# Memory keys behind the latent heads' transposes, paired products at a stage's entry, residual sums with priority

## The chip, the cores and the metric

The kernel runs on one core of a Trainium2 chip. The metric is the device time of one execution in microseconds (us). Engines are named as in the profile: PE is the matrix engine's multiplication, PEld its weight load, DVE the vector engine, ACT the scalar engine, POOL the GpSimd engine, SP the engine whose queue issues the weight loads.

## The reference, cut to what matters

Two transformer blocks run one after the other on an input of 256 tokens by 1024 features, in fp32. In short:

```
x = x + 0.5 * swiglu(norm(x), W1)                   # stage ffn1, hidden width 2816
z = norm(x) @ w_in + b_in                           # stage mix: sliding-window attention, mLSTM
x = x + merged(attention, mlstm, gates) @ w_out
x = x + 0.5 * swiglu(norm(x), W2)                   # stage ffn2
x = norm(x)
x = x + concat(gated_linear_attention, latent_attention) @ w_out_2     # stage mix2
x = x + cross_attention(norm(x), norm(mem)) @ xa_w_o                   # part xa of mix2
x = x + (silu(conv3(norm(x) @ w_gate)) * (norm(x) @ w_up)) @ w_down    # stage ffn3
```

In mix2 the latent attention has 8 heads of 96 query and key features. The cross attention of xa has 4 heads of 128; its keys are a product of the 256 memory tokens with a 1024 by 512 matrix and do not depend on x. The norm's gain is multiplied into x before a product; the factor of the norm that differs by token is applied to the product.

## The kernel before, in words

The activations lie transposed, as eight feature tiles `x[0]` to `x[7]` of 128 features by 256 tokens. Every fp32 matrix product is made from halves: an operand is split into a high part that the fast fp32 format holds, and the remainder. `x_done(d)` (line 462) splits feature tile d with the next norm's gain: ACT writes the high part (line 480), DVE the low part (line 481). `halves` (line 346) does the same for a piece of weights: ACT writes `wh` (line 354), DVE writes `wl` (line 355); there are six buffers of each, a piece holds 1024 columns, and in mix2 and the first two products of ffn3 it is written in two instructions of 512 columns. Raw weights come by SP's queue into three buffers `wr`.

`mm3` (line 374) is one step of a product over one feature tile: two instructions, one of 512 columns and one of 256 (lines 382 and 383). `lin_t` (line 391) makes two output tiles j = 0, 1 over eight feature tiles k, 16 such steps, into one buffer of the PSUM pool `mm`, which has two. `lin_n` (line 401) makes a product with tokens as rows, by three instructions of 512 columns for each feature tile and token block (lines 387 to 389). The pool `at` has four PSUM banks; scores, transposes, small sums and the first product of a stage use it.

`lin_first` (line 418) makes the first product of a stage, whose feature tiles have only just been written: for both j the first six feature tiles, then the last two. In ffn2 and ffn3 that is the gate product `g0`, followed by `lin_t` for the up product `u0`; in mix it is `aq00`, followed by `aq01`. At the end of mix, `wo0` to `wo3` (line 914) multiply the merged heads `gs`, which are written two feature tiles at a time as the products `pm0` to `pm3` end (lines 906 to 910); `joined` (line 534) empties a product's PSUM by ACT (line 540) and DVE (line 541).

In `mix2_heads`, `turned(hp)` (line 1163) transposes the queries `q` and keys `kn` of one pair of latent heads on PE (line 1169, four transposes each) and copies them out as `qT` (DVE, line 1172) and `kT` (ACT, line 1174). `scores(qT, hp)` multiplies them (lines 1184, 1185), and `values` the rows after the softmax. The source has turned(0), scores(0), turned(1), then the products og and uv, scores(1), turned(2), the product gv, then `xa_memory` and values(0), and then `xa_keys` (line 1376): the memory keys `xk`, a `lin_n` of 48 instructions over eight feature tiles, squares (line 1386), a reciprocal root on POOL, a multiplication (line 1390). `xa_turn` transposes the result on PE (line 1399).

In `xa` (line 1407), `values(0)` (line 1468) stands right behind the memory values `xv` (line 1405). Then come turn(1) (line 1460), norm(3) (line 510), scores(3) (line 1442), and the output products xo0 and xo1, each followed by four additions to x (lines 1507 and 1513) and `x_done`.

The instructions are not issued in the order of the source. A planner simulates the program with its own times for each instruction, and gives each engine a fixed list: of what is ready in its simulation, the instruction that stands first in the source. On the chip each engine works off its list and waits on semaphores.

Of the kernel before, what the change touches and what calls it, by code (L numbers as in the profile page):

```python
# [2 lines left out]

# [1 line left out]

# [10 lines left out]
ALU = mybir.AluOpType  # L16
# [171 lines left out]
class Builder:  # L188
# [209 lines left out]
                self.mm3(ps[:, j, :], hv[j][0][:, k, :], hv[j][1][:, k, :], xs[k], k == 0, k == kt - 1)  # L398
        return ps

    def lin_n(self, key, n, xs, kt=KD, pool=None):

        ps = [(pool or self.bank)() for _ in range(TB)]
        for k, kk, runs in n_runs(n, kt):
            raw = self.wraw(f"{key}.{k}")
            for s, m in runs:
                hi, lo = self.halves(raw[:, s * n:(s + m) * n])
                for i in range(m):
                    q = k + s + i
                    for b in range(TB):  # L410
                        self.mm3n(ps[b][:, :n], xs[q][:, 0, b * P:b * P + P], xs[q][:, 1, b * P:b * P + P],
                                  hi[:, i * n:i * n + n], lo[:, i * n:i * n + n], q == 0, q == kt - 1)
        return ps

    def xtiles(self, k):
        return self.xp.tile([P, 2, T], F32R, tag=f"xs{k}", name=self.n(f"xs{k}"))

    def lin_first(self, key, xs, raw=None):


        ps = [self.pa() for _ in range(2)]
        if raw is None:
            hv = self.wcols(key, 2)
            for ks in (range(6), range(6, 8)):
                for j in range(2):
                    for k in ks:
                        self.mm3(ps[j], hv[j][0][:, k, :], hv[j][1][:, k, :], xs[k], k == 0, k == 7)
        else:
            for q in range(4):
                for d in (2 * q, 2 * q + 1):  # L430
                    self.x_done(d)
                    xs.append(self.halved[d])
                hl = [t[:, :512].rearrange("p (j k c) -> p j k c", j=2, k=2) for t in self.halves(raw[:, q * 512:q * 512 + 512])]
                for j in range(2):
                    for k in range(2):
                        self.mm3(ps[j], hl[0][:, j, k, :], hl[1][:, j, k, :], xs[2 * q + k],
                                 q + k == 0, q + k == 4)
        return ps


# [106 lines left out]
    def ffn(self, f, half, nxt=None, conv=False, last=False, first=False, mem=False):  # L547
# [3 lines left out]
        with self.phase("ffn") as fp:  # L551
            ft = lambda shape, tag, bufs=1, dt=F32: fp.tile(shape, dt, tag=tag, name=self.n(tag), bufs=bufs)
            xs = [] if first else self.split_x()
            ahl = ft([P, 2, KF, T], "ahl", dt=F32R)
            pairs = {}

            def products(pr):
                if pr == 0:
                    pg = self.lin_first(f"{f}g{pr}", xs, self.first if first else None)
                else:  # L560
                    pg = self.lin_t(f"{f}g{pr}", xs)
                if conv:
                    s = ft([P, 2, T + 2], "g", 2)
                    nc.vector.memset(s[:, :, 0:2], 0.0)
                    self.joined(pg, s[:, :, 2:])
                else:
                    s = ft([P, 2, T], "s", 2)
                    self.joined(pg, s)
                a = ft([P, 2, T], "a", 2)
                self.joined(self.lin_t(f"{f}u{pr}", xs, early=first and pr == 0), a)  # L570
                pairs[pr] = s, a

            if not first:
                acc = self.squares(self.x2)
            products(0)
            if first:
                acc = self.squares(self.x2, True)
            rN, _ = self.rinv_n(self.mean(acc, "ms"))
            products(1)
            self.fine = 1  # L580
            if first:
                self.ip = fp
                self.consts2()
                self.rope_tables()
            r = self.by_token(rN)
            rh = ft([P, T], "rh")
            nc.vector.tensor_scalar(rh, r, 0.5 if half else 1.0, None, ALU.mult)
            for pr in range(KF // 2):
                if pr > 1:
                    products(pr)  # L590
                s, a = pairs.pop(pr)
                if conv:
                    g, s = s, ft([P, 2, T], "s", 2)
                    nc.vector.tensor_tensor(g[:, :, 2:], g[:, :, 2:], self.bc2(r), ALU.mult)
                    for j in range(2):
                        w = [self.col("cw3", 22 * t + 2 * pr + j) for t in range(3)]
                        nc.scalar.activation(s[:, j, :], g[:, j, 2:], AF.Identity, scale=w[2], bias=self.col("cb3", 2 * pr + j))
                        for t in (1, 0):
                            nc.vector.scalar_tensor_tensor(s[:, j, :], g[:, j, t:T + t], w[t], s[:, j, :], ALU.mult, ALU.add)
                else:  # L600
                    nc.vector.tensor_tensor(s, s, self.bc2(r), ALU.mult)
                nc.scalar.activation(s, s, AF.Silu)
                nc.vector.tensor_tensor(a, s, a, ALU.mult)
                self.split(ahl[:, :, 2 * pr:2 * pr + 2, :], a)
            if mem:
                self.xa_norm()
            if nxt is not None:
                self.then(nxt)
            for dp in range(KD // 2):
                short = dp == KD // 2 - 1  # L610
                ps = self.pm()[:, :, :T if short else 2 * T]
                for k0, kt in balanced(KF, 8):
                    hv = self.wcols(f"{f}d{dp}.{k0}", 2, kt)
                    for j in range(2):
                        for k in range(kt):
                            q = k0 + k
                            self.mm3(ps[:, j, :], hv[j][0][:, k, :], hv[j][1][:, k, :], ahl[:, :, q, :],
                                     q == 0, q == KF - 1)
                y = ft([P, 2, T], "dy", 2)
                if not short:  # L620
                    self.joined(ps, y, rh)
                    nc.vector.tensor_tensor(J(self.x2[dp]), J(self.x2[dp]), y, ALU.add)
                for j in range(2):
                    d = dp * 2 + j
                    if short:
                        nc.vector.tensor_tensor(y[:, j, :], ps[:, j, :], rh, ALU.mult)
                        nc.vector.tensor_tensor(x[d], x[d], y[:, j, :], ALU.add)
                    if nxt is not None:
                        self.x_done(d)
                    if last:  # L630
                        nc.sync.dma_start(self.out[:, d, :], x[d])


    def mix(self):
# [4 lines left out]
        with self.phase("mix") as mp:  # L639
# [11 lines left out]
                    nc.scalar.activation(t[:, j, :], t[:, j, :], AF.Identity, bias=self.col("bin", bias + j))  # L651
                return [t[:, j, :] for j in range(2)]

            aqs = {"aq00": product("aq00", "aq00", self.lin_first("aq00", xs)), "aq01": product("aq01", "aq01")}
            rN, _ = self.rinv_n(self.mean(acc, "ms"))
            aqs["aq10"] = product("aq10", "aq10")
            rB = self.by_token(rN)
# [253 lines left out]
            self.then(self.col("gff2", 0, 8))  # L911
            for dp in range(4):
                short = dp == 3
                ps = self.lin_t(f"wo{dp}", [gs[:, :, k, :] for k in range(8)], one=short)
                xd = J(self.x2[dp])
                for i in range(0 if short else 2):
                    nc.vector.scalar_tensor_tensor(xd, ps[:, :, i * T:i * T + T], 0.5, xd, ALU.mult, ALU.add)
                for j in range(2):
                    if short:
# [115 lines left out]
    def mix2_heads(self, mp, ot, xs, ms):  # L1035
# [127 lines left out]
        def turned(hp):  # L1163
            qT = []
            for name, src in (("qT", q), ("kT", kn)):
                pt = self.pa()
                for i in range(2):
                    for b in range(TB):
                        nc.tensor.transpose(pt[:96, i * T + b * P:i * T + b * P + P], src[:, b, 2 * hp + i, :], self.ident)
                t = mt([96, 512], name, bufs=2)  # L1170
                if name == "qT":
                    V.tensor_scalar(t, pt[:96, :], self.gqk[:96], None, ALU.mult)
                else:
                    nc.scalar.activation(t, pt[:96, :], AF.Copy)
                qT.append(t)
            return qT

        def scores(qT, hp):
# [22 lines left out]
        def values(hp, Ss):  # L1201
# [13 lines left out]
            ms[4 + hp] = ot([P, 2, T], f"mla{hp}", dt=F32R)  # L1215
            self.split(ms[4 + hp], po[:, :T])

        q0 = turned(0)
        S0 = scores(q0, 0)
        q1 = turned(1)  # L1220
# [24 lines left out]
        ts = self.xa_memory()  # L1245
        values(0, S0)
        xkT = ot([P, 4, T], "xkT")
        kk = self.xa_keys(ts, g2)


        pt = self.bank()
# [121 lines left out]
        self.nc.vector.tensor_copy(self.rm, rm)  # L1373
        self.nc.vector.tensor_scalar(self.vm, vm, P * EPS, None, ALU.mult)

    def xa_keys(self, ts, mt):

        nc = self.nc
        V = nc.vector
        ps = self.lin_n("xk", 512, ts)  # L1380
        ks = self.tmp([P, TB, 4], "ks", bufs=1)
        rk = self.tmp([P, TB, 4], "xrk", bufs=1)
        kk = [mt([P, 4, P]) for b in range(TB)]
# [23 lines left out]
    def xa(self, mp, xkT, ts):  # L1407
# [80 lines left out]
        scores(2)  # L1488
        xv = mt([P, TB, 512], "xv")
        self.xa_values(ts, xv)  # L1490
        values(0)
        turn(1)
        norm(3)
        scores(3)
        values(1)
        hv = self.wcols("xo0", 4, 4, per=2)
        ps = [self.bank()[:, :T] for _ in range(4)]
# [5 lines left out]
        out(ps, hv, [(2, j) for j in range(4)])  # L1503
        values(3)
        out(ps, hv, [(3, j) for j in range(4)])
        for j in range(4):
            V.tensor_tensor(x[j], ps[j], x[j], ALU.add)
            self.x_done(j)
        hv = self.wcols("xo1", 4, 4, per=2)
        ps = [self.pa()[:, :T] for _ in range(4)]  # L1510
        out(ps, hv, [(k, j) for j in range(4) for k in range(4)])
        for j in range(4):
            V.tensor_tensor(x[4 + j], ps[j], x[4 + j], ALU.add)
            self.x_done(4 + j)


STAGES = ("ffn1", "mix", "ffn2", "mix2", "ffn3")
# [47 lines left out]
```

## Time and profile before

| what | value |
|---|---|
| median of 3 runs | 1020.57 us (1017.5, 1020.57, 1023.98) |
| the profiled execution's own time | 1020.17 us |
| its span, first to last instruction | 1018.5 us |
| PE busy | 990.7 us, 97% of the span, 5870 instructions |
| PEld busy | 857.9 us, 84% |
| DVE busy | 741.2 us, 73% |
| ACT busy | 595.9 us, 59% |
| POOL busy | 65.9 us, 6% |
| mean granted TensorE clock | 0.993 |
| read from HBM | 170.72 MB |

Busy time is the time in which an engine has at least one instruction at work. PE's instructions overlap: a matmul of 512 columns counts about 0.39 us, while the next one starts after about 0.23 us. So what a matmul costs is read from the distance of two starts, and a wait from PE's idle time. A granted clock of 1.0 is 2.4 GHz, and 0.5 is 1.2 GHz.

### The profile page before, as it was taken

To read this page: it belongs to the slowest core of one execution; us is meant where nothing else is said; L and a number is where in the kernel's file an instruction comes from. 1 tells how busy PE (TensorE), PEld (TensorE's weight loads), DVE (VectorE), ACT (ScalarE), POOL (GpSimd) and SP (SyncE) were. 2 spreads that over 40 slices of the span, in tenths; PEclk is the share of its full clock that TensorE was granted. 3 is DMA by queue.
4 is the path that set the end of the run, shared out by engine and by line. 5 is a ranking of instruction groups with operands and counts; after the bars stand their busy time and mean duration, and the time that the engine had idled before them with its cause. 6 is when DMAs were issued, how large, how long until landed. Compare 5 with 4: busy or idle time off the path is not lost.

```text
span 1018.5 us, 15397 instructions
## 1 busy us (share of the span) xinstructions
PE 990.7 (97%) x5870; PEld 857.9 (84%) x5870; DVE 741.2 (73%) x1286; ACT 595.9 (59%) x1036; POOL 65.9 (6%) x200
## 2 busy tenths in 40 slices
PE   6999999999999999999999999999899999999998
PEld 5888888988677788889888888988788888888887
DVE  7877766567986578777777856768867678888652
ACT  5755544458864655555655644659755467666541
POOL 4100000010000010001000200012001201000000
PEclk9999999999999999999999999999899999999999
DMA  6755545545345245545555655365106335555450
GB/s 231 272 179 193 182 170 186 203 152 212 125 134 184 96 129 202 199 171 174 198 175 201 208 179 189 133 243 202 47 3 247 125 111 196 190 181 181 172 191 21
DMA packets 28507, 172.77 MB, mean 170 GB/s; under 512 B 3712, under 2 KB 5008, under 8 KB 10128
## 3 DMA queue, kind: packets, MB, share of 16 engines
q1 hardware_dynamic: 26640, 169.88, 48.0%
q10 hardware_dynamic: 1728, 1.88, 0.8%
q8 instruction: 46, 0.75, 0.3%
q14 instruction: 29, 0.24, 0.1%
q0 software_dynamic: 64, 0.02, 0.0%
HBM read 170.72 MB, written 1.05 MB: 169 GB/s over the span
## 4 chain that ended last, share of the span: by engine, by line
PE 86%; DVE 5%; DMA 3%; ACT 2%; POOL 2%; issue 2%; DVEq 0%; ACTq 0%
PE mm L382 40%; PE mm L383 20%; PE mm L379 3%; PE mm L378 3%; PE mm L380 3%; DVE wl L355 2%; PE mm L387 2%; PE mm L388 2%; PE mm L389 2%; DMA wr<-in_wts 2%; PE at L382 1%; ACT wh L354 1%; PE at L733 1%; PE at L693 1%; PE at L383 1%
## 5 line engine op out<-in xcount | busy, mean ns | idle before, releaser
L355 DVE TENSOR_TENSOR wl<-wr,wh 128x1024 fp32r<-128x1024 f32 (+5 forms) x380 | 394.1, 1049 | 202.2 <-ACT wh L354 201.3
L354 ACT ACTIVATE wh<-wr 128x1024 fp32r<-128x1024 f32 (+5 forms) x380 | 341.2, 915 | 323.5 <-PE mm L382 191.1
L382 PE MATMUL mm<-xs,wh 128*128 128x512 f32 x1264 | 446.2, 398 | 1.4 <-DVE a L541 1.3
L383 PE MATMUL mm<-xs,wl 128*128 128x256 f32 x1264 | 354.1, 280 | 0.0
L382 PEld LDWEIGHTS mm<-xs,wh 128*128 128x128 f32 x1264 | 237.6, 188 | 59.0 <-issue 2.2
L383 PEld LDWEIGHTS mm<-xs,wl 128*128 128x128 f32 x1264 | 238.7, 189 | 0.5 <-issue 0.3
L382 PE MATMUL mm<-ahl,wh 128*128 128x512 f32 x396 | 139.2, 397 | 0.0
L383 PE MATMUL mm<-ahl,wl 128*128 128x256 f32 x396 | 110.7, 280 | 0.0
L382 PEld LDWEIGHTS mm<-ahl,wh 128*128 128x128 f32 x396 | 74.4, 188 | 18.1
L383 PEld LDWEIGHTS mm<-ahl,wl 128*128 128x128 f32 x396 | 74.7, 189 | 0.0
L388 PE MATMUL mm<-wl,xs 128*128 128x512 f32 (+2 forms) x160 | 61.1, 382 | 0.0
L387 PE MATMUL mm<-wh,xs 128*128 128x512 f32 (+2 forms) x160 | 60.9, 381 | 0.0
L389 PE MATMUL mm<-wh,xs 128*128 128x512 f32 (+2 forms) x160 | 60.7, 379 | 0.0
L382 PE MATMUL mm<-b,wh 128*128 128x512 f32 x128 | 45.5, 395 | 0.0
L379 PE MATMUL mm<-ahl,wh 128*128 128x256 f32 x132 | 37.3, 283 | 0.0
L378 PE MATMUL mm<-ahl,wh 128*128 128x256 f32 x132 | 37.3, 283 | 0.0
L380 PE MATMUL mm<-ahl,wl 128*128 128x256 f32 x132 | 37.3, 283 | 0.0
L383 PE MATMUL mm<-b,wl 128*128 128x256 f32 x128 | 36.5, 285 | 0.0
L382 PE MATMUL at<-xs,wh 128*128 128x512 f32 x64 | 26.2, 449 | 9.6 <-DVE xs L481 9.6
L388 PEld LDWEIGHTS mm<-wl,xs 128*128 128x128 f32 x160 | 30.1, 188 | 6.2 <-issue 1.5
L387 PEld LDWEIGHTS mm<-wh,xs 128*128 128x128 f32 x160 | 30.1, 188 | 6.1 <-issue 1.1
L389 PEld LDWEIGHTS mm<-wh,xs 128*128 128x128 f32 x160 | 30.1, 188 | 5.8 <-issue 0.8
(539 smaller groups left out, 1450.4 us busy)
## 6 DMA issues: line engine op xcount, KB each, us to landing
wr<-in_wts SPq DMA_DIRECT2D x141, 1024.0 KB, 4.9
wr<-in_wts SPq DMA_DIRECT2D x12, 768.0 KB, 4.3
wr<-in_wts SPq DMA_DIRECT2D x6, 512.0 KB, 4.1
wr<-in_memt SPq DMA_DIRECT2D x2, 1024.0 KB, 5.8
wr<-in_wts SPq DMA_DIRECT2D x2, 864.0 KB, 4.2
wr<-in_wts SPq DMA_DIRECT2D x6, 256.0 KB, 5.6
bb<-in_rows ACTq DMA_DIRECT2D x6, 256.0 KB, 4.6
wr<-in_wts SPq DMA_DIRECT2D x2, 544.0 KB, 3.5
```

Of the source, the lines that this page charges most:

```text
L354: nc.scalar.activation(hi[:, i:i + m], v[:, i:i + m], AF.Copy)
L355: nc.vector.tensor_tensor(lo[:, i:i + m], v[:, i:i + m], hi[:, i:i + m].bitcast(F32), ALU.subtract)
L378: mm(ps, wh, xs[:, 0, :], start=start, stop=False)
L379: mm(ps, wh, xs[:, 1, :], start=False, stop=False)
L380: mm(ps, wl, xs[:, 0, :], start=False, stop=stop)
L382: mm(ps, wh, xs, start=start, stop=False)
L383: mm(ps[:, T:], wl, xs[:, 0, :], start=False, stop=stop)
L387: mm(ps, xh, wh, start=start, stop=False)
L388: mm(ps, xh, wl, start=False, stop=False)
L389: mm(ps, xl, wh, start=False, stop=stop)
L693: nc.tensor.matmul(ps[h][:, i * nk:i * nk + nk], aq[p][g * per + i][hs, b * P:b * P + P], ak[p][hs, 0:nk], start=True, stop=True)
L733: nc.tensor.matmul(po[64 * h:64 * h + 64, :], av[:, kb, kv * 64:kv * 64 + 64], pTs[2 * kb + h], start=kb == 0, stop=kb == b)
```

## The change

It has four parts.

1. `xa_keys` gets a list: the instructions of the key product for feature tiles 2 to 4 get an edge on PE from the last transpose of turned(0), those for tiles 5 to 7 one from the last transpose of turned(1). The edge (`issue_after`) has no semaphore; it binds the planner's order.
2. `lin_first` takes one or two products. It walks the feature tiles in three groups, 0 to 3, 4 and 5, 6 and 7, and in each group does both j of the first product and both j of the second. The first product goes into two banks of `at`, the second into a buffer of `mm`. ffn2 and ffn3 pass g0 and u0, mix passes aq00 and aq01. `wo0` now goes this way alone; its sum into x is made by four additions of 256 columns instead of two of 512. The very first product of ffn1 keeps its code under the name `lin_start`.
3. In xa, `values(0)` stands behind scores(3).
4. The additions to x and `x_done` after xo0 and xo1 stand under `high_priority(offset=300)`: the planner ranks them as if they stood 300 instructions earlier in the source.

```
-    def lin_n(self, key, n, xs, kt=KD, pool=None):
+    def lin_n(self, key, n, xs, kt=KD, pool=None, behind=None):
...
-                    for b in range(TB):
-                        self.mm3n(ps[b][:, :n], xs[q][:, 0, b * P:b * P + P], xs[q][:, 1, b * P:b * P + P],
-                                  hi[:, i * n:i * n + n], lo[:, i * n:i * n + n], q == 0, q == kt - 1)
+                    with self.tc.issue_after(behind[q].ins) if behind and behind[q] else nullcontext():
+                        for b in range(TB):
+                            self.mm3n(ps[b][:, :n], xs[q][:, 0, b * P:b * P + P], xs[q][:, 1, b * P:b * P + P],
+                                      hi[:, i * n:i * n + n], lo[:, i * n:i * n + n], q == 0, q == kt - 1)
...
+    def lin_first(self, keys, xs):
+
+        hvs = [self.wcols(key, 2) for key in keys]
+        out = [[self.pa() for _ in range(2)] if i == 0 else self.pm() for i in range(len(keys))]
+        for ks in ((0, 1, 2, 3), (4, 5), (6, 7)):
+            for hv, ps in zip(hvs, out):
                 for j in range(2):
                     for k in ks:
-                        self.mm3(ps[j], hv[j][0][:, k, :], hv[j][1][:, k, :], xs[k], k == 0, k == 7)
...
+                        self.mm3(ps[j] if isinstance(ps, list) else ps[:, j, :], hv[j][0][:, k, :], hv[j][1][:, k, :],
+                                 xs[k], k == 0, k == 7)
+        return out
...
+                elif pr == 0:
+                    pg, pu = self.lin_first([f"{f}g0", f"{f}u0"], xs)
...
-                self.joined(self.lin_t(f"{f}u{pr}", xs, early=first and pr == 0), a)
+                self.joined(pu or self.lin_t(f"{f}u{pr}", xs, early=first and pr == 0), a)
...
-            aqs = {"aq00": product("aq00", "aq00", self.lin_first("aq00", xs)), "aq01": product("aq01", "aq01")}
+            ps = self.lin_first(["aq00", "aq01"], xs)
+            aqs = {key: product(key, key, p) for key, p in zip(("aq00", "aq01"), ps)}
...
-                ps = self.lin_t(f"wo{dp}", [gs[:, :, k, :] for k in range(8)], one=short)
+                gk = [gs[:, :, k, :] for k in range(8)]
+                if dp == 0:
+                    (ps,) = self.lin_first(["wo0"], gk)
+                    for i in range(2):
+                        for j in range(2):
+                            nc.vector.scalar_tensor_tensor(x[j], ps[j][:, i * T:i * T + T], 0.5, x[j], ALU.mult, ALU.add)
+                else:
+                    ps = self.lin_t(f"wo{dp}", gk, one=short)
...
-        kk = self.xa_keys(ts, g2)
+        kk = self.xa_keys(ts, g2, [None] * 2 + [self.turns[0]] * 3 + [self.turns[1]] * 3)
...
-        values(0)
         turn(1)
         norm(3)
         scores(3)
+        values(0)
         values(1)
...
-        for j in range(4):
-            V.tensor_tensor(x[j], ps[j], x[j], ALU.add)
-            self.x_done(j)
+        with self.tc.high_priority(offset=300):
+            for j in range(4):
+                V.tensor_tensor(x[j], ps[j], x[j], ALU.add)
+                self.x_done(j)
```

The second such loop, for `x[4]` to `x[7]`, is changed in the same way, and `turned` appends its last transpose to `self.turns`.

## Rows read from the trace of the kernel before

**Rows 1.** Waits of PE over the whole run: total, times, longest, in us.

```profile
PE at L382 <- DVE xs L481: 9.6, 2, 7.3
```

**Rows 2.** Timeline of PE, then DVE, at wo0: start, us, idle time before.

```profile
441.06 0.50 PE L382 MATMUL mm<-vs,wh 128*128 128x512 f32 x1 [1.51 <-DVE z L541]
...
443.24 0.39 PE L382 MATMUL mm<-vs,wh 128*128 128x512 f32 x1
...
443.59 0.39 PE L382 MATMUL mm<-vs,wh 128*128 128x512 f32 x1
...
444.38 0.50 PE L382 MATMUL mm<-vs,wh 128*128 128x512 f32 x1 [0.28 <-DVE vs L478]
...
440.32 0.68 DVE L541 TENSOR_TENSOR z<-mm,z 128x512 f32<-128x512 f32 x1
```

**Rows 3.** Busy time by stretch of mix2: length, PE, PEld, DVE, ACT, POOL, granted clock, DMA.

```profile
700.00:730.00 30.00, 26.51 (x159) 22.22 (x158) 27.24 (x74) 25.12 (x65) 3.43 (x15) 0.89 0.38 141
715.50:719.20 3.70, 0.21 (x3) 0.04 (x1) 3.70 (x13) 3.23 (x19) 0.00 (x0) 0.94 0.00 0
719.20:725.80 6.60, 6.60 (x27) 5.82 (x28) 5.15 (x22) 4.56 (x16) 2.37 (x11) 0.52 0.25 82
```

**Rows 4.** Timeline of PE in mix2, from the first pair's key transposes to the third's.

```profile
709.70 0.60 PE L1169 MATMUL at<-ident,kn 128*96 128x128 f32 x4
...
713.12 0.39 PE L389 MATMUL mm<-wh,xs 128*128 128x512 f32 x1
713.35 0.38 PE L1184 MATMUL at<-kT,qT 96*128 96x128 f32 x2
...
714.66 0.60 PE L1169 MATMUL at<-ident,q 128*96 128x128 f32 x4
...
719.19 0.77 PE L1184 MATMUL at<-kT,qT 96*128 96x128 f32 x2 [3.49 <-DVE qT L1172]
...
721.88 1.06 PE L1169 MATMUL at<-ident,q 128*96 128x128 f32 x4
```

**Rows 5.** The tile kn, 700 to 725 us: its last writes, count, ns, first and last start.

```profile
L1131 DVE TENSOR_TENSOR kn<-kp,rkp x2: 420/421/422, 703.9 to 704.2; 128x256 f32<-128x256 f32 x2
```

**Rows 6.** Groups of DVE instructions in 700 to 730 us: the low weight parts.

```profile
L355 DVE TENSOR_TENSOR wl<-wr,wh 128x512 fp32r<-128x512 f32 x13 | 8.6, 688 | 0.0
```

**Rows 7.** Timelines of DVE and PE: the memory keys' multiplication, and their transposes.

```profile
723.65 1.27 DVE L1390 TENSOR_TENSOR g2k<-mm,xrk 128x512 f32<-128x512 f32 x2
...
730.35 1.04 PE L1399 MATMUL mm<-ident,g2k 128*128 128x128 f32 x8
```

**Rows 8.** Timeline of PE in xa, behind the memory values.

```profile
803.53 0.67 PE L1468 MATMUL at<-pT,xv 128*128 128x256 f32 x2 [1.14 <-DVE xv L1405]
804.04 0.60 PE L1460 MATMUL at<-ident,S 128*128 128x128 f32 x4
...
805.79 1.46 PE L1468 MATMUL at<-pT,xv 128*128 128x256 f32 x6
```

**Rows 9.** Busy time by stretch at the entry of ffn3, columns as in rows 3.

```profile
820.90:823.40 2.50, 0.24 (x3) 0.04 (x2) 2.50 (x6) 2.50 (x7) 0.00 (x0) 1.00 0.00 0
...
824.50:828.00 3.50, 3.50 (x13) 3.02 (x12) 3.50 (x9) 2.54 (x6) 0.00 (x0) 0.51 0.67 279
```

**Rows 10.** Groups of DVE and ACT instructions, 818 to 828 us: busy, mean ns, idle before.

```profile
L355 DVE TENSOR_TENSOR wl<-wr,wh 128x512 fp32r<-128x512 f32 x8 | 5.3, 685 | 0.0
L481 DVE SCALAR_TENSOR_TENSOR xs<-x,cols,xs 128x256 fp32r<-128x256 f32 x6 | 2.7, 480 | 0.0
...
L480 ACT ACTIVATE xs<-x,cols 128x256 fp32r<-128x256 f32 x8 | 3.6, 492 | 0.0
```

**Rows 11.** Timeline of DVE: the four additions behind xo0.

```profile
818.12 1.42 DVE L1507 TENSOR_TENSOR x<-mm,x 128x256 f32<-128x256 f32 x4 [3.15 <-PE mm L380]
```

**Rows 12.** Busy time by stretch at the entries of mix and ffn2, columns as in rows 3.

```profile
215.00:226.00 11.00, 11.00 (x67) 9.67 (x66) 5.96 (x12) 3.97 (x8) 3.11 (x11) 1.00 0.68 234
...
465.00:480.00 15.00, 15.00 (x89) 13.15 (x88) 10.59 (x17) 9.24 (x16) 0.05 (x1) 1.00 0.37 127
```

More of the change, by code (lines that the diff above doesn't have):

```diff
@@ L1 @@
 import math
-from contextlib import ExitStack, contextmanager
+from contextlib import ExitStack, contextmanager, nullcontext
 import numpy as np
@@ L416, in xtiles, with lin_start @@
         return self.xp.tile([P, 2, T], F32R, tag=f"xs{k}", name=self.n(f"xs{k}"))
[L418 to L424, printed above, removed]
+    def lin_first(self, keys, xs):
[3 more added lines that the diff above has]
+            for hv, ps in zip(hvs, out):
                 for j in range(2):
                     for k in ks:
-                        self.mm3(ps[j], hv[j][0][:, k, :], hv[j][1][:, k, :], xs[k], k == 0, k == 7)
[L428 to L437, printed above, removed]
+                        self.mm3(ps[j] if isinstance(ps, list) else ps[:, j, :], hv[j][0][:, k, :], hv[j][1][:, k, :],
+                                 xs[k], k == 0, k == 7)
+        return out
+    def lin_start(self, raw, xs):
+        ps = [self.pa() for _ in range(2)]
+        for q in range(4):
+            for d in (2 * q, 2 * q + 1):
+                self.x_done(d)
+                xs.append(self.halved[d])
+            hl = [t[:, :512].rearrange("p (j k c) -> p j k c", j=2, k=2) for t in self.halves(raw[:, q * 512:q * 512 + 512])]
+            for j in range(2):
+                for k in range(2):
+                    self.mm3(ps[j], hl[0][:, j, k, :], hl[1][:, j, k, :], xs[2 * q + k],
+                             q + k == 0, q + k == 4)
         return ps
@@ L557, in products @@
             def products(pr):
-                if pr == 0:
-                    pg = self.lin_first(f"{f}g{pr}", xs, self.first if first else None)
+                pu = None
+                if pr == 0 and first:
+                    pg = self.lin_start(self.first, xs)
+                elif pr == 0:
+                    pg, pu = self.lin_first([f"{f}g0", f"{f}u0"], xs)
                 else:
@@ L913, in mix @@
                 short = dp == 3
-                ps = self.lin_t(f"wo{dp}", [gs[:, :, k, :] for k in range(8)], one=short)
+                gk = [gs[:, :, k, :] for k in range(8)]
+                if dp == 0:
+                    (ps,) = self.lin_first(["wo0"], gk)
+                    for i in range(2):
+                        for j in range(2):
+                            nc.vector.scalar_tensor_tensor(x[j], ps[j][:, i * T:i * T + T], 0.5, x[j], ALU.mult, ALU.add)
+                else:
+                    ps = self.lin_t(f"wo{dp}", gk, one=short)
                 xd = J(self.x2[dp])
-                for i in range(0 if short else 2):
+                for i in range(0 if short or dp == 0 else 2):
                     nc.vector.scalar_tensor_tensor(xd, ps[:, :, i * T:i * T + T], 0.5, xd, ALU.mult, ALU.add)
@@ L1168, in turned @@
                     for b in range(TB):
-                        nc.tensor.transpose(pt[:96, i * T + b * P:i * T + b * P + P], src[:, b, 2 * hp + i, :], self.ident)
+                        end = nc.tensor.transpose(pt[:96, i * T + b * P:i * T + b * P + P], src[:, b, 2 * hp + i, :], self.ident)
                 t = mt([96, 512], name, bufs=2)
@@ L1175, in turned @@
                 qT.append(t)
+            self.turns.append(end)
             return qT
@@ L1216, in values @@
             self.split(ms[4 + hp], po[:, :T])
+        self.turns = []
         q0 = turned(0)
@@ L1374, in xa_norm, with xa_keys @@
         self.nc.vector.tensor_scalar(self.vm, vm, P * EPS, None, ALU.mult)
-    def xa_keys(self, ts, mt):
+    def xa_keys(self, ts, mt, behind):
         nc = self.nc
         V = nc.vector
-        ps = self.lin_n("xk", 512, ts)
+        ps = self.lin_n("xk", 512, ts, behind=behind)
         ks = self.tmp([P, TB, 4], "ks", bufs=1)
@@ L1511, in xa @@
         out(ps, hv, [(k, j) for j in range(4) for k in range(4)])
-        for j in range(4):
-            V.tensor_tensor(x[4 + j], ps[j], x[4 + j], ALU.add)
-            self.x_done(4 + j)
+        with self.tc.high_priority(offset=300):
+            for j in range(4):
+                V.tensor_tensor(x[4 + j], ps[j], x[4 + j], ALU.add)
+                self.x_done(4 + j)
 STAGES = ("ffn1", "mix", "ffn2", "mix2", "ffn3")
```

## The prediction, made before the change was run

> **What bounds the kernel now.** I read the page first: PE is busy for 990.7 of 1018.5 us. The change removes no PE work, so it can return only PE's idle time and half-speed time. The next view is the list of what PE waited for. Its largest entry, 9.6 us in two waits for the low part of an activation tile, is 7.3 us at the start of the kernel, which the change does not touch, and 2.3 us at the entry of ffn3 [rows 1]. The timeline then gives each wait its place. At wo0 PE stands 1.51 us until line 541 has emptied the last pm product, and 0.28 us for the last tile of gs [rows 2]. In mix2 it stands 3.49 us for the second pair's qT [rows 4], and in xa 1.14 us for the memory values [rows 8].
>
> The third view is busy time by stretch with the granted clock. After the mix2 wait PE runs 6.6 us at 0.52 of its clock, the lower level but for the edges, and after the ffn3 wait 3.5 us at 0.51 [rows 3, 9]. Elsewhere around these places it is 1.0. The same eight score instructions show what that costs: 1.31 us from 713.35 to 714.66, but 2.69 us from 719.19 to 721.88 [rows 4]. So the two stretches cost 6.6 x 0.48 = 3.2 us and 3.5 x 0.49 = 1.7 us. After the 1.51 us wait at wo0 two steps are 0.35 us apart [rows 2], which is PE's pitch where it does not wait; a wait that short did not slow the clock.
>
> **The sum** is made against the profiled execution's own 1020.17 us, 1.7 us more than its span and 0.4 us below the median of the three runs.
>
> **wo0.** Now it uses two `at` banks. I read the 1.51 us as the second wo product waiting for the `mm` buffer that pm3 held: line 541 is that buffer's last reader. With wo0 out of the pool of two, the second wo takes the other buffer at once. While gs is being written, PE then has the six early tiles of wo0, 12 steps of 0.35 us, or 4.2 us, and as much again of the next product. I take the wait for line 541 as gone, -1.5, and leave the 0.28. Four additions (the like four take 1.42 us [rows 11]) replace two of 0.68 us [rows 2], 0.1 us more on DVE; PE's next product covers that, and without the cover it is the upper end. Ends: -1.8 and +0.1.
>
> **Memory keys.** Between the first pair's key transposes at 709.70 and its scores at 713.35 there is room for some 15 of the 48 key instructions at 0.23 us [rows 4], so the list of before runs two thirds of the keys ahead of those transposes, although kn is complete at 704.6 us [rows 5] already. With the edges, only tiles 0 and 1, 12 instructions, may come first. On the chip kn is there when PE gets to it, at about 705 (709.70 less 20 instructions of 0.23 us). Tiles 2 to 4, 18 instructions, or 4.1 us, then lie over the copying of the first pair, and tiles 5 to 7, again 4.1 us, over that of the second pair, where PE stood 3.49 us. If nothing else is late, that returns 3.5 and the clock's 3.2, 6.7 us. What is late next is DVE: it is busy all 3.70 us of the wait, and 27.24 of the 30 us from 700 to 730 [rows 3]. The same DVE work can move up by its idle time, 2.8 us, plus what can be put off, such as a low weight part of 0.69 us for a later product [rows 6]. I take 2.8 + 0.7 = -3.5, nearest to DVE's row, not to PE's. The key transposes at 730.35 have slack, as the multiplication before them ends at 724.9 [rows 7]: keys that end up to 5.4 us later cost nothing. Ends: -6.7, and a loss that the last rival prices.
>
> **values(0) in xa.** Before it now stand turn(1), norm(3) and scores(3), which take 804.04 to 805.79, 1.75 us [rows 8], more than the wait of 1.14. I take -1.1. Ends: -1.1 and 0, since the instructions are the same.
>
> **Entry of ffn3.** PE has no work from 820.9 to 823.4 while DVE and ACT are full [rows 9]. DVE mixes eight low weight parts of 0.685 us into eight additions of 0.36 us [rows 11] and eight low activation parts of 0.48 us [rows 10]; the first such part is late for that. With priority the first tile needs 818.1 + 0.4 + 0.49 on ACT + 0.48 = 819.5, before PE runs dry. All additions and low parts end at 818.1 + 8 x 0.84 = 824.8. PE has 8 steps on the first four tiles of g0 to 823.7, 4 on the next two to 825.1 and 4 on the last to 826.5; u0's first low weights are there at 825.5. What is queued behind the sums on DVE is thus u0's four low weight parts, 2.7 us; PE would wait for them only if g0's steps were not there. I leave 0.6 us of the 2.3 for tiles that come singly, -1.7, and count the clock as held, -1.7: -3.4. Ends: -4.0, and +1.0 if PE waits for the 2.7 us in place of 1.7.
>
> **Other entries.** At mix and ffn2 PE is busy without a gap [rows 12], so pairing returns nothing. It holds four of six weight buffers for 32 steps, 11.2 us, and leaves two pieces, 5.6 us of PE work, as cover; DVE is busy for 10.6 of 15 us there, so I cost it at nothing. With the cover gone it is a piece of 1.4 us (twice rows 6) at each of two entries, 2.8. No DMA is added, and no queue is passed: SP's loads only follow the freed buffers.
>
> Sum: -1.5 - 3.5 - 1.1 - 3.4 = -9.5, so 1020.17 - 9.5 = **1010.7 us**.
>
> **The rivals.**
>
> *DVE stays the limit.* Both large waits fall where DVE is full [rows 3, 9], and priority only changes which of its products comes late: u0's weights instead of x. The planner may also do already what the pairing asks. Then wo0 gives 1.5, mix2 1.5, ffn3 1.7 without the clock, xa nothing: 4.7, so 1015.5. Against it: the low weight parts can be put off.
>
> *All of it comes back.* 1.8 + 6.7 + 1.1 + 4.0 = 13.6, so 1006.6. For it: the waits are single places, and the clock falls only behind the two longest. Against it: DVE's 27.24 of 30 us.
>
> *The keys stand behind late transposes* (slower). PE takes its list in order: it stood 3.49 us for qT and took nothing from behind. If the planner's times leave the first pair's key transposes at 709.70, PE idles 18 x 0.23 = 4.1 us before them and the clock falls as it did behind 3.49 us, 3.2 us; this replaces the removed 6.7, +0.6. The last 18 keys end at 710.1 + 4.1 + 3.2 + 1.3 (scores) + 0.9 (transposes) + 4.1 = 723.7, 10.3 us later than now. The slack is 5.4, so PE stands 4.9 us at the key transposes and the clock falls again, 3.2. mix2 then loses 0.6 + 8.1 = 8.7, and against wo0, xa and ffn3 (-6.0) the kernel is 2.7 slower: 1022.9. With the upper ends of ffn3 and of the other entries it is 1030.1. It decides from the point where those transposes come 4 us or more after 705. Against it: kn is ready at 704.6, and q earlier.
>
> The Trainium skill has a rule that bears on this rival, in "TensorE: Matmul & The Clock Gate", section "Step-by-step: what each phase is for": weight loads may be pulled ahead, but matmuls stay in program order. By that rule, an edge that comes too late cannot be worked around on the chip, and the time would be this rival's. The trace agrees as far as it goes, with the 3.49 us idle.
>
> **How the numbers follow.** Chances: forecast 0.45, DVE stays the limit 0.25, all of it 0.15, late transposes 0.15. About 1% is what a measurement of this kernel can tell from no change, 10.2 us: the bounds are 1010.4 and 1030.8. The forecast lies on the first, so I give half of it to each side: faster 0.22 + 0.15 = 0.37. Slower by that much is the worse half of the last rival, 0.08; the rest, 0.55, is within. The range leaves out a tail of the full gain and the worse half of the last rival: 1005 to 1022. The forecast's own range is 1007.5 to 1014.
>
> **What would show it.** Right: no PE idle above 1 us at 441, 719, 803 and 821, the clock at 1.0 through mix2 and ffn3's entry, kn's first transposes some 4 us earlier against the gv product, and the first low part within 1.5 us of the first sum. Wrong: a new PE wait for kn, qT or kT ahead of the keys, one for wl at ffn3's entry or behind a pair at mix or ffn2, or a mix2 wait that only changed its name to another DVE product.

## The result and the profile after

The changed kernel takes 1031.32 us (median of 8 runs, 1025.41 to 1033.62) where the kernel before, beside it, takes 1020.15 us (8 runs, 1013.62 to 1023.98). The ratio is 1.0104, with a 95% interval of 1.0082 to 1.0126: slower by about 1%, where 1010.7 was predicted. The profiled execution is the shortest of the eight, 1025.41 us, with a span of 1023.7 us. So it shows less of the loss than the median; the last section has a likely reason.

First the list of what PE waited for, after (line: total in us, times, longest). Lines have moved: the sums of the norm are L516 (L510 before), the broadcast of its factor L532 (L526), the low activation part L487 (L481), the scores L1202 (L1184).

```profile
PE at L382 <- DVE xs L487: 9.6, 2, 7.3
PE at L532 <- POOL rN L462: 7.2, 2, 3.7
PE at L383 <- DVE wl L355: 1.6, 2, 1.0
PE mm L1285 <- ACT g2k L1275: 1.2, 1, 1.2
PE mm L1285 <- DVE am L1292: 1.0, 1, 1.0
PE at L1224 <- DVE S L1214: 1.0, 1, 1.0
PE at L1360 <- DVE czog L1354: 0.9, 2, 0.7
...
PE at L1202 <- ACT kT L1191: 0.6, 1, 0.6
```

Three waits of before have left the list: 1.51 us at wo0 [rows 2], 3.49 us for qT [rows 4], 1.14 us for xv [rows 8]. The wait at ffn3's entry still stands in the first line, as large as in [rows 1]. New is the second line: PE waits for POOL, which the prediction does not mention, at the entries of ffn2 and ffn3. The last five are new too: in mix2 the one long wait has become several short ones.

This is ffn2's entry, from the timelines of PE and then of POOL and DVE (start, duration, idle before and its end):

```profile
470.25 0.50 PE L516 MATMUL at<-ones,acc 128*128 128x1 f32 x4
...
475.21 0.40 PE L382 MATMUL mm<-xs,wh 128*128 128x512 f32 x1
...
479.44 1.22 PE L532 MATMUL at<-ident,rN 128*128 128x128 f32 x4 [3.72 <-POOL rN L462]
...
481.10 0.63 PE L382 MATMUL mm<-xs,wh 128*128 128x512 f32 x1
481.74 0.63 PE L382 MATMUL mm<-xs,wh 128*128 128x512 f32 x1
...
472.89 1.02 POOL L451 TENSOR_SCALAR rN<-rNv 128x2 int32<-128x2 int32 x1 [102.65 <-PE mm L382]
474.00 1.05 POOL L453 TENSOR_TENSOR rs<-rN 128x2 f32<-128x2 f32 x1
475.13 0.20 POOL L454 TENSOR_TENSOR rs<-rs,rNv 128x2 f32<-128x2 f32 x1
...
475.68 1.10 POOL L456 TENSOR_TENSOR rN<-rs,rN 128x2 f32<-128x2 f32 x1
476.86 1.14 POOL L457 TENSOR_TENSOR rs<-rN 128x2 f32<-128x2 f32 x1
...
479.19 0.19 POOL L462 TENSOR_TENSOR rN<-rs,rN 128x2 f32<-128x2 f32 x1
...
472.64 2.36 DVE L355 TENSOR_TENSOR wl<-wr,wh 128x1024 fp32r<-128x1024 f32 x2
...
475.51 2.44 DVE L355 TENSOR_TENSOR wl<-wr,wh 128x1024 fp32r<-128x1024 f32 x2
```

PE's list puts the broadcast of the norm's factor behind only 28 matmuls that follow the sums; before, 51 stood between them (26 and 58 in ffn3). The sums end at 470.75, POOL's chain of eleven small steps at 479.38. PE has run out of work ahead of it at 475.7 and stands 3.72 us. Then its steps are 0.64 us apart instead of 0.35: the clock is at its lower level from 479.4 to 482.5. The same happens in ffn3:

```profile
848.70 1.22 PE L532 MATMUL at<-ident,rN 128*128 128x128 f32 x4 [3.47 <-POOL rN L462]
```

The stretches after, in us from the span's start (columns as in [rows 3]):

```profile
479.40:482.50 3.10, 3.06 (x11) 2.77 (x12) 1.38 (x3) 0.38 (x1) 0.00 (x0) 0.51 0.72 301
...
718.00:724.80 6.80, 4.63 (x35) 3.56 (x35) 6.80 (x26) 6.30 (x30) 1.60 (x4) 1.00 0.01 2
724.80:735.00 10.20, 9.16 (x58) 7.36 (x57) 8.01 (x25) 4.50 (x17) 2.39 (x8) 0.50 0.14 51
825.30:827.80 2.50, 0.28 (x3) 0.07 (x1) 2.50 (x6) 2.50 (x7) 0.00 (x0) 1.00 0.00 0
847.70:854.50 6.80, 5.80 (x19) 5.13 (x20) 1.88 (x4) 0.39 (x1) 0.69 (x4) 0.50 0.52 198
```

and before, behind the wait for qT:

```profile
718.70:725.50 6.80, 6.31 (x25) 5.78 (x26) 5.35 (x21) 4.29 (x16) 2.37 (x11) 0.50 0.24 80
```

Against these and [rows 9]: DVE is full ahead of the waits in mix2 as it was, and the lower clock behind them lasts 10.2 us, not 6.8. At ffn3's entry PE is idle for the same length with DVE and ACT full. The clock did not fall behind that wait this time, but behind the next one, for the factor. In mix2 itself, in PE's timeline:

```profile
706.48 0.60 PE L1186 MATMUL at<-ident,kn 128*96 128x128 f32 x4
...
718.26 0.39 PE L1202 MATMUL at<-kT,qT 96*128 96x128 f32 x2
...
722.05 1.23 PE L1224 MATMUL at<-ident,S 128*128 128x128 f32 x6 [1.00 <-DVE S L1214]
724.45 1.37 PE L1285 MATMUL mm<-qz,g2k 64*64 64x64 f32 x16 [1.17 <-ACT g2k L1275]
726.86 1.57 PE L1285 MATMUL mm<-qz,g2k 64*64 64x64 f32 x16 [1.04 <-DVE am L1292]
```

The first pair's key transposes come at 706.48, against 709.70 in [rows 4], and the second pair's scores follow without a wait. Up to here the forecast holds, but for 0.64 us that the first pair's scores wait for kT. The next three products of DVE and ACT are then late, by 1.00 + 1.17 + 1.04 = 3.21 us.

To see where each part of the change acts, I took the start of PE's n-th matmul in every profile and subtracted that of the kernel before. All kernels have 5870 matmuls. The columns are what was lost (+) or won (-) within a stage, in us:

```
                 wo0   ffn2 entry    mix2   xo parts   ffn3 entry
                                               of xa
n from          2300         2640    3940       4620         4700
n to            2560         2800    4300       4700         5000
after           -1.7         +4.8    +3.3       -0.6         +3.2
pairs_only       0.0         +5.4    -1.4        0.0         +2.7
a_nopairs       -1.7         -0.1    +3.3       -0.6         -0.2
a_hold          -1.7         -0.3    +3.3       -0.6         +0.1
a_nokeys        -1.7         +5.4    -1.0       -0.6         +5.2
keys_only        0.0         +0.3    +3.2       -0.2         +0.1
wo_val          -1.7         +0.3    -0.7       -0.6         +0.1
fix_only         0.0          0.0    -0.1        0.0         -1.5
wo_val_fix      -1.7         +0.3    -1.5       -0.6         -2.8
wo_val_fix2     -1.7         +0.4    -1.0       -0.6         -4.1
wo_val_fix_k3   -1.7         +0.3    +4.4       -0.4         -0.8
```

The first row sums to +9.0 us; the ratio of 1.0104 is 10.6. The other rows are the experiments.

### The profile page after: what moved, and what is told of

Same layout as the page of the kernel before. It is cut to its first block, busy times and chain, and to the rows that moved or that the text cites. A ratio compares the mean times of both kernels' runs of the same rounds, so it can differ in the third digit from the quotient of the medians.

```text
span 1023.7 us, 15404 instructions
## 1 busy us (share of the span) xinstructions
PE 992.2 (97%) x5870; PEld 861.0 (84%) x5870; DVE 741.6 (72%) x1288; ACT 595.3 (58%) x1036; POOL 72.9 (7%) x200
## 4 chain that ended last, share of the span: by engine, by line
PE 86%; DVE 5%; ACT 3%; POOL 3%; DMA 2%; issue 2%; DVEq 0%; POOLq 0%; ACTq 0%
PE mm L382 39%; PE mm L383 20%; PE mm L378 3%; PE mm L379 3%; PE mm L387 3%; PE mm L380 3%; PE mm L388 3%; PE mm L389 3%; DVE wl L355 2%; PE at L382 1%; ACT wh L354 1%; DMA wr<-in_wts 1%; PE at L743 1%; PE at L703 1%; PE at L383 1%
## 5 line engine op out<-in xcount | busy, mean ns | idle before, releaser
L355 DVE TENSOR_TENSOR wl<-wr,wh 128x1024 fp32r<-128x1024 f32 (+5 forms) x380 | 392.9, 1045 | 198.6 <-ACT wh L354 194.3
```

The costliest lines, as they stand in the source:

```text
L355: nc.vector.tensor_tensor(lo[:, i:i + m], v[:, i:i + m], hi[:, i:i + m].bitcast(F32), ALU.subtract)
```

## The experiments

Each was timed in alternation with the kernel before; ratios are to that, with 95% intervals. The kernels without the pairing still contain the new `lin_first`, which walks a single product in the three groups. In ffn2 that is worth next to nothing: -0.1 to +0.4 in the table.

**The pairing.** Theory 1: it costs two waits for the norm's factor, because paired products are both unfinished while they hold four of the six weight buffers. The planner then finds nothing else ready and lists the broadcast early. The rival: the time goes elsewhere. Four kernels bear on it.

`a_nopairs` is the changed kernel with one product at a time at the three entries:

```
-                    pg, pu = self.lin_first([f"{f}g0", f"{f}u0"], xs)
+                    (pg,) = self.lin_first([f"{f}g0"], xs)
...
-            ps = self.lin_first(["aq00", "aq01"], xs)
+            (ps,) = self.lin_first(["aq00"], xs)
```

> The changed kernel with one product at a time at the entries of mix, ffn2 and ffn3 (wo0, keys, values(0), priority stay). Theory 1 (pairing costs the time: with four of six weight buffers held, the planner has no product ready and lists the broadcast of the norm's factor after 28 and 26 matmuls instead of 51 and 58, so PE stands 3.7 us for POOL at each of two entries and the clock falls): about 8.5 us under the changed kernel, 1022 to 1024, no PE wait for POOL at ffn2 and ffn3, no clock fall there. Rival (the memory keys cost the time, the waits for POOL only replace waits that were there): within 2 us of the changed kernel, 1029 to 1033.

Measured: 1019.93 us, 1.0013 (0.9986 to 1.0040). The waits for POOL at the two entries are gone, as theory 1 has it.

`a_hold` is the changed kernel, pairs kept, with the broadcast bound behind the second gate and up products in ffn2 and ffn3:

```
-            r = self.by_token(rN)
+            with nullcontext() if first else self.tc.issue_after(self.end.ins):
+                r = self.by_token(rN)
```

Here `self.end` is the last matmul of products(1).

> The changed kernel with pairing kept, but the broadcast of the norm's factor in ffn2 and ffn3 put behind the last matmul of the second pair of products on PE. Theory 1 in its planner form (the weights are there on the chip, only the list is wrong): the waits for POOL go, no wait for weights comes, about 8 us under the changed kernel, 1022 to 1024. Rival form (the weights are really late, because four of six buffers are held): PE waits 2 to 4 us for low weight parts at each entry in place of POOL, 1027 to 1031.

Measured: 1019.3 us, 1.0003 (0.9977 to 1.0030). In its PE timeline, and then POOL's, the broadcast comes later and no wait stands before it, although POOL's chain is as long as in the changed kernel:

```profile
470.53 0.50 PE L516 MATMUL at<-ones,acc 128*128 128x1 f32 x4
...
481.66 0.60 PE L532 MATMUL at<-ident,rN 128*128 128x128 f32 x4
...
473.15 1.02 POOL L451 TENSOR_SCALAR rN<-rNv 128x2 int32<-128x2 int32 x1 [102.65 <-PE mm L382]
...
479.56 0.20 POOL L462 TENSOR_TENSOR rN<-rs,rN 128x2 f32<-128x2 f32 x1
```

`pairs_only` is the kernel before with the pairing alone; its diff is the reverse of that of a_nopairs.

> The kernel before with pairing at mix, ffn2 and ffn3 alone (no edges for keys, wo0, values(0) and priority as before). Theory 1: both waits for POOL come, with the clock fall, 8 us over the kernel before, 1027 to 1030. Rival (keys cost the time): 1019 to 1022.

Measured: 1027.39 us, 1.0091 (1.0061 to 1.0122). Its list of PE's waits has both kinds:

```profile
PE at L532 <- POOL rN L462: 7.2, 2, 3.7
PE at L1197 <- DVE qT L1184: 3.5, 1, 3.5
```

So the pairing alone makes nearly the whole loss, and one edge on the broadcast, with the pairing kept, removes it: the early place in the list causes the loss. With the edge the pairing costs nothing and returns nothing (a_hold in the table, -0.3 and +0.1). That the planner lists the broadcast early because buffers are held is seen in its lists alone, which were not timed. Seven weight buffers of each kind fit beside the pools of the mix stage only with two raw ones in place of three. In the changed kernel's list 57 and 58 matmuls then stand between the sums and the broadcast, and with six and two, 30 and 26.

**The memory keys.** `a_nokeys` is the changed kernel without the edges, `keys_only` the kernel before with them alone:

```
-        kk = self.xa_keys(ts, g2, [None] * 2 + [self.turns[0]] * 3 + [self.turns[1]] * 3)
+        kk = self.xa_keys(ts, g2, None)
```

> The changed kernel without the edges that put the memory keys behind the transposes. Theory 2 (in mix2 the wait for qT became several shorter waits for DVE and ACT with a longer half-speed stretch, a net loss of 3.4 us): 3 to 4 us under the changed kernel, 1027 to 1029. Rival (the forecast's: the edges give a gain that was lost elsewhere): 3 us over it, 1034 to 1036. If the edges make no difference: 1031.

Measured: 1027.36 us, 1.0089 (1.0059 to 1.0118). The difference from the changed kernel's 1.0104 is too small for these intervals, so the term was measured alone:

> The kernel before with the memory keys' edges alone (tiles 2 to 4 behind turned(0), 5 to 7 behind turned(1)). The prediction's term: 3.5 us less, ratio 0.9966, the wait for qT gone and nothing in its place. Theory 2 (VectorE and ScalarE set this stage; the wait is cut into several shorter ones at L1224 and L1285, and TensorE's clock stays at its lower level for longer): between 1 us less and 2 us more, ratio 0.999 to 1.002, with three waits of 1.0 to 1.4 us between 718 and 727 and half clock for 7 to 10.2 us there.

Measured: 1021.79 us, 1.0051 (1.0026 to 1.0076), slower than both theories had it. Its waits in mix2:

```profile
PE at L1226 <- ACT pT L1221: 1.3, 1, 1.3
PE mm L1280 <- ACT g2k L1270: 1.2, 1, 1.2
PE at L1219 <- DVE S L1209: 1.0, 1, 1.0
```

In the table, the kernels with all edges lose 3.2 to 3.3 us in mix2 against the kernel before, and those without win up to 1.5 us. Part of that spread is the clock. Behind mix2's waits it is at the lower level for 10.2 us in after, a_nopairs, a_hold and wo_val_fix_k3, and for 6.8 in keys_only. Without edges it is 3.4 us in pairs_only, a_nokeys, wo_val, wo_val_fix and wo_val_fix2, and 6.8 in before and fix_only. The stretch in keys_only and in wo_val_fix2:

```profile
726.00:732.80 6.80, 6.46 (x30) 4.60 (x31) 4.24 (x16) 2.61 (x11) 0.99 (x5) 0.50 0.17 67
```

```profile
718.60:722.00 3.40, 3.40 (x17) 3.01 (x16) 2.59 (x12) 1.96 (x9) 2.19 (x11) 0.50 0.35 139
```

But keys_only has the lower clock for as long as before, and loses 3.2 us all the same. The whole stretch of the table, from matmul 3940 to 4300, in before, after and keys_only:

```profile
694.32:753.20 58.88, 54.42 (x361) 44.87 (x360) 47.74 (x142) 43.96 (x124) 10.12 (x35) 0.94 0.25 90
```

```profile
696.10:758.30 62.20, 56.77 (x361) 45.65 (x360) 48.05 (x142) 43.08 (x124) 11.73 (x35) 0.92 0.24 85
```

```profile
695.70:757.80 62.10, 56.18 (x362) 44.39 (x361) 47.72 (x143) 42.97 (x124) 11.70 (x35) 0.95 0.24 86
```

PE is idle for 4.5, 5.4 and 5.9 us of it. So with the small ones for kT and `czog` (L1360), the waits add up to 1.0 and 1.5 us more than those of before. PE's work at half speed, 6.3, 9.2 and 6.5 us, costs half of itself: 1.4 us more in after, 0.1 in keys_only. What remains of the loss, 0.9 and 1.6 us, I did not trace to a cause.

**The small moves.** `wo_val` is the kernel before with wo0 by feature tiles and values(0) behind scores(3).

> The kernel before with the two small moves alone: wo0 by feature tiles, values(0) behind scores(3); no keys, no pairs, no priority. The prediction's terms: 1.5 and 1.1 us less, ratio 0.9975. The trace after gave 2.1 to 2.3 and 0.65 to 1.1, so 2.8 to 3.4 less. Rival: both come back later at a wait that DVE sets, ratio 1.000, with the total of the wait list for DVE larger by as much.

Measured: 1016.32 us, 1.0007 (0.9982 to 1.0032): no gain that this measurement shows, and the lower end of the interval holds only 1.8 us. The table has -1.7 at wo0 in all seven kernels that contain it beside after, and 0.0 in the three that don't; values(0) has -0.4 to -0.6, against -0.2 to 0.0. PE's waits for DVE did not grow, so the rival's sign is absent. The terms, 2.3 us together, are there in the profiles, and the timing of this kernel does not confirm them; I did not resolve this.

**The order at ffn3's entry.** I built one kernel twice, the kernel before with the new `lin_first` for single products, with and without the priority. The lists of all five engines are the same, instruction by instruction, and so are those of the changed kernel with and without it. DVE's timeline after shows the order of before, low weight parts (L355) ahead of the first low activation part (L487):

```profile
822.58 1.42 DVE L1527 TENSOR_TENSOR x<-mm,x 128x256 f32<-128x256 f32 x4 [3.13 <-PE mm L380]
823.91 0.68 DVE L355 TENSOR_TENSOR wl<-wr,wh 128x512 fp32r<-128x512 f32 x1
...
826.11 1.28 DVE L355 TENSOR_TENSOR wl<-wr,wh 128x512 fp32r<-128x512 f32 x2
827.31 0.48 DVE L487 SCALAR_TENSOR_TENSOR xs<-x,cols,xs 128x256 fp32r<-128x256 f32 x1
```

In the kernel before, the four low parts between the sums and the first low activation part are u0's, whose steps PE could do without while it has those of g0. So I put the intended order into effect by edges:

```
+                with self.behind(lows[5]) if pr == 0 and f == "f3" else nullcontext():
+                    pu = pu or self.lin_t(f"{f}u{pr}", xs, early=first and pr == 0)
...
+                    with self.behind(lows[7]) if pr == 1 and f == "f3" else nullcontext():
+                        pg = self.lin_t(f"{f}g{pr}", xs)
```

`behind(lows[d])` binds ACT's and DVE's instructions in its block behind the split of feature tile d. `wo_val_fix` adds this to wo_val, `fix_only` to the kernel before; `wo_val_fix2` has tiles 3 and 5 in place of 5 and 7.

> As wo_val, and at ffn3's entry the splits of u0's weights (ACT and DVE) put behind the split of xs tile 5, those of g1's behind tile 7: what the priority was written for. If the order of DVE's list makes the wait for xs (2.43 us at 825.29, with 1.7 us of lower clock behind it) then 2.4 to 4.1 us less than wo_val, ratio 0.990 to 0.994 of the kernel before. Rival: DVE is full there and only the names change; PE then waits for u0's weights (L382 <- wl L355 grows by 2 us or more), 0 to 1 us less than wo_val.

> The kernel before with nothing but ffn3's order put in effect (ACT's and DVE's splits of u0's weights behind that of xs tile 5, g1's behind tile 7). In wo_val_fix this entry lost its wait of 2.43 us and its stretch of lower clock, 4.0 us, and gave 1.2 us back at a later PSUM wait: 2.8 us less, ratio 0.9972. If the stage gives all back at g's eviction: 1.000.

> As wo_val_fix with u0's weights behind xs tile 3 and g1's behind tile 5, so two to four weight splits earlier. If the late weights make the wait of 2.4 us for g's PSUM bank at 849.9, then up to 1.2 us less than wo_val_fix (ratio 0.994 to 0.996 of before). Rival: six weight splits (6 x 0.60 = 3.6 us on DVE) stand ahead of xs tiles 4 and 5, PE has only 4 x 2 steps of 0.35 us = 2.8 us to do before it needs them, and a wait for xs of 0.8 us or more comes back: 1 to 3 us more than wo_val_fix.

Measured: wo_val_fix 1015.82 us, 0.9973 (0.9945 to 1.0002); fix_only 1018.9 us, 1.0007 (0.9987 to 1.0027); wo_val_fix2 1012.7 us, 0.9952 (0.9932 to 0.9972). The last beats both kernels. In its busy times by stretch PE has no idle time at the entry, where its first step on xs starts at 817.95, and in DVE's timeline the first low activation part starts 2.0 us after the first sum, not 4.7:

```profile
818.00:824.00 6.00, 6.00 (x35) 5.20 (x35) 6.00 (x15) 6.00 (x13) 0.00 (x0) 1.00 0.15 34
...
815.12 1.42 DVE L1537 TENSOR_TENSOR x<-mm,x 128x256 f32<-128x256 f32 x4 [3.13 <-PE mm L380]
816.45 0.75 DVE L1544 TENSOR_TENSOR x<-at,x 128x256 f32<-128x256 f32 x2
817.11 0.87 DVE L493 SCALAR_TENSOR_TENSOR xs<-x,cols,xs 128x256 fp32r<-128x256 f32 x2
```

Neither the clock nor PE stops there any more, and ffn3's entry wins 4.1 us. With the later edges it is 4.0 us at first, but u0's and g1's splits then come late, and in wo_val_fix PE waits for `g`:

```profile
PE mm L382 <- DVE g L581: 2.4, 1, 2.4
```

That gives 1.2 us back in wo_val_fix and 2.5 in fix_only, where PE waits for `g` twice. Both kernels fall short of the gain expected of them, and fix_only shows none in its timing. (The wait that the expectations give as 2.43 us is 2.27 in the traces of after and wo_val.) The rival that I had for wo_val_fix2, a new wait for tiles 4 and 5, did not come.

`wo_val_fix_k3` adds edges for key tiles 5 to 7 alone.

> As wo_val_fix, with only key tiles 5 to 7 put behind turned(1)'s transposes, 2 to 4 left as before: 9 blocks of three products over the gap ahead of scores(1) and none ahead of scores(0). By theory 2 the qT wait of 3.5 us is shortened by 2 us or more and what follows gives most of it back: 0 to 1.5 us less than wo_val_fix. By the prediction's term: 3 us less.

Measured: 1020.68 us, 1.0032 (1.0009 to 1.0056), slower than wo_val_fix, though theory 2 had up to 1.5 us less than that and the prediction's term 3 us less. Three tiles' edges cost at least as much as six: the wait for qT is gone and 1.7 us for kT, 1.4 for g2k and 1.3 for pT have come in its place.

## Why the prediction was wrong

**Other entries: 0 forecast for the pairing, +8.0 measured** (4.8 at ffn2 and 3.2 at ffn3; at mix no wait came). This step failed, and it makes most of the loss: without the pairing the kernel is as fast as before (a_nopairs, 1.0013), though not faster. The step asked which weight piece PE could lack, priced that at 2.8 us and cost it at nothing. What PE lacked was listed work: with g0 and u0 both open, the next listed instruction waits for a chain on another engine. Neither this step nor the one on ffn3's entry read the distance in PE's list from the sums to the broadcast, nor POOL's chain. That chain took 5.76 us before as well (479.95 to 485.71), and 51 matmuls just covered it: the broadcast started at 485.76. The two waits measure 3.72 + 3.47 us, and the clock falls behind both.

The Trainium skill has the rule for it, in "TensorE: Matmul & The Clock Gate", section "Step-by-step: what each phase is for": matmuls stay in program order. I used it for the keys alone. The trace agrees: with the broadcast in front, PE did nothing for 3.72 us.

**Memory keys: -3.5 forecast, +3.2 to +3.3 measured.** The failed step is that DVE's work "can move up by its idle time, 2.8 us, plus what can be put off". DVE did become full, 6.80 of 6.80 us from 718.0. But the products of DVE and ACT are wanted one after another, and PE met S and am (DVE) and g2k (ACT) late instead of qT. This is the sign of being wrong that the prediction named last, a wait that only changed its name; it counted as "DVE stays the limit" with 1.5 us won, and I had no case in which the new waits add up to more than the old one, or in which the clock loses more behind them. The slower rival, late transposes, did not occur: they came at 706.48, about where I had put them.

**Entry of ffn3: -3.4 forecast, 0 from the priority.** The failed step is "with priority the first tile needs ... 819.5". The priority changed no list. The additions stand ahead of u0 in the source already; the weights come first because they are ready first, which a rank does not change (argued from the planner's rule; that the lists are equal is shown). The size was about right for the order itself: with edges it is -4.1 in the table.

**wo0: -1.5 forecast, -1.7 measured.** Right, in cause too: the wait is gone, and of 2.3 us won at first 0.6 are given back. **values(0): -1.1 forecast, -0.6 measured**, by the columns of the table; its wait is gone, and of 1.3 us won at first 0.7 are given back.

So the forecast and all three rivals were wrong on the pairing: none has the wait for POOL, and none prices the other entries above 2.8 us. The chance of 0.08 for slower by over 1% came from late transposes alone, and their worst end was 1030.1.

## What to carry to other kernels

When instruction order is planned, a change that keeps buffers busy for longer can also move what is listed behind it: look for the next instruction that waits on a long chain elsewhere, and count the work listed in front of it, before and after. Where an engine is full ahead of a wait, giving PE other work there can move the wait to the next products, as in mix2; what helped at ffn3 was a different order on the full engine. And a priority is worth nothing until the lists show that it changed them.

## What the runs showed of the hardware that I had not expected

**Small POOL steps stretch when DVE writes low weight parts.** A root chain is eleven steps on 128x2 values (L451 to L462). In the changed kernel such a step takes about 0.20 us, or 0.5 to 1.2. Of the 24 long ones, 23 start inside an instruction of line 355 and one inside line 612, which also has two SBUF inputs, and each ends about 0.05 us after that instruction does: the steps at 472.89, 474.00, 475.68 and 476.86 above lie in the four parts of 472.64 to 477.95. None of the 86 short ones starts inside line 355. Over all twelve profiles, all 234 steps that start inside line 355 are long; of 176 that start inside a DVE instruction on two tensors of which one is in PSUM, such as those of line 547, none is. By an estimate from these times, the chain without it would take about 3 us (11 x 0.20 and ten gaps of 0.08) in place of 6.5, and most of the new wait would not be there. The Trainium skill, "SBUF — State Buffer", section "Who interferes with whom", says that a DVE instruction with two SBUF inputs contends with a GpSimd instruction that reads SBUF, and that such contention is an exclusive lock. The trace agrees, with these counts and ends; no run here took the low weight parts away from the chain.

**The same matmuls run at two paces at the same granted clock.** In a stretch of ffn3 that is alike in both kernels, before and then after:

```profile
880.00:960.00 80.00, 80.00 (x454) 69.38 (x453) 67.59 (x98) 50.31 (x70) 0.00 (x0) 1.00 0.52 178
```

```profile
880.00:960.00 80.00, 80.00 (x464) 69.94 (x463) 70.19 (x104) 52.66 (x73) 0.00 (x0) 1.00 0.53 184
```

PE is busy throughout and the clock is 1.00 in both, but 464 matmuls fit against 454, 2.2% more: one step of 512 and 256 columns takes 0.347 us instead of 0.353. A profile keeps one pace for a hundred us or more and then may change. Over a span this makes several us. The profiled execution after ran at the quicker pace here and from 60 to 160 us, which may be why it is below its median; the other seven have no trace. The table by stage leaves most of it out, as it has only the stretches around the edits. I found no cause.

**The clock does not always fall behind the same wait.** Behind the wait of 2.3 us at ffn3's entry it fell for 3.4 us in before and in six other kernels, and not in after (wait from 825.6 to 827.8, clock 1.0 until 847.7).
